# Time-mixing units of a hybrid RWKV-7 / Conformer trunk: key tiles made for both heads at once, chunk-end scaling and row moves on ScalarE, bonus in one matmul

## The chip, the cores and the metric

The kernel runs on one core of one Trainium2 chip. The metric is the device time of one execution in microseconds; lower is better. Before the change it is 2194.57 us, the median of three runs.

## The reference, cut to what matters

The program is a two-layer trunk over 512 tokens of width 1024. Each layer is a SwiGLU feed-forward block, a mixer, and another feed-forward block; the first mixer is RWKV-7 time mixing, the second a causal convolution module. The change touches time mixing alone: for each of 16 heads of 64 channels a 64 x 64 state S is carried through the tokens.

```python
kk = k * k_k, normalised per head
k  = k * (1 + (a - 1) * k_a)
a_vec, b_vec = -kk, kk * a
# per token t and head:
sa = S @ a_t
S  = S * w_t + outer(sa, b_t) + outer(v_t, k_t)
y_t = S @ r_t
# after the scan:
y = group_norm(y) * ln_gain + ln_bias
bonus = sum(r * k * r_k over the head) * v
out = ((y + bonus) * g) @ w_out
```

## The kernel before, in words

Activations stand transposed, channels on the 128 partitions and tokens along the free dimension. Large products run on TensorE in fp32r with operands split in a rounded part and a rest (names ending in h and l), three matmuls for each product. Weights come by DMA in tiles `wr` of eight blocks; ScalarE casts each to `wh`, VectorE makes the rest `wl = wr - wh`, and TensorE uses both. Two buffers of each exist.

Time mixing is cut into eight units. Unit p holds two pairs of heads for one half of the tokens (four chunks of 64 tokens for each pair); units 0 to 3 are the first half of the sequence, 4 to 7 the second. A unit has a front part (tiles for all eight chunks) and a back part (a chain over four chunk steps). Rows 0 to 63 of a tile belong to the first head of a pair, rows 64 to 127 to the second.

Front part: `ka` holds kk and r times the running decay `pt` (a product for each head and each half of the unit, on GpSimd); `bkc` holds b (VectorE) and k (GpSimd) divided by the decay, the two in different column order for the two heads; `bkh` is `bkc` times the decay at the chunk's end `pc` (GpSimd). Matmuls `Gb` and `Gk` of `bkc` and `ka` give the matrices within a chunk; VectorE masks `Gk` into the free rows of `ka`, and inverts the triangular part with many small instructions on `tm` and `lt`, and with matmuls `X` and `D` into `tt`.

Back part: `tk` transposes `bkh` into `bk`; `tv` centres v, and ScalarE puts it into `uv` and `mv`. Each of the four steps is a chain of three groups of matmuls into `z`: from `ka` and `mv`, a copy, from `tt`, two copies into `uv`, from `bk` and `uv`, and an addition into the next columns of `mv`. Then `y` is made from `ka`, `mv`, `Gb` and `uv`. The bonus `bo` is a product with a block-diagonal matrix of ones, from `k2` = r k r_k, which is split in `k2..h` (ScalarE) and `k2..l` (GpSimd), so two fp32r matmuls.

The order of all instructions is fixed before the run by a planner in the kernel (class `Sched`): it lists instructions on the engines from its own table of costs, a due order (the program's order), numbers of buffers, and rules for the port that VectorE and GpSimd share. Where it sees TensorE about to wait it puts in fillers, `warm`: matmuls of 128 x 512 on a constant tile whose result nobody reads. An engine then works strictly in that order; where the chip is slower than the table, the whole queue behind waits. `copier` means that the planner picks ScalarE or VectorE for a copy, `both` VectorE or GpSimd.

Between the steps of units TensorE is given projections (`k`, `r`, `v`), the output projection `wo` and the feed-forward block that follows (`f1g`, `f1u`, `f1d`).

## Time and profile before

| | |
|---|---|
| three runs | 2194.26, 2194.57, 2195.81 us |
| profiled execution: time, span | 2190.93 us, 2189.1 us |
| TensorE busy | 2137.0 us, 98% of the span |
| VectorE busy | 1303.9 us, 60% |
| ScalarE busy | 854.8 us, 39% |
| GpSimd busy | 521.2 us, 24% |
| stretch with the units' steps | 470 to 930 us of the span |

The profiled execution is one run, 0.17% below the median of the three. Busy time of TensorE includes the tail of each pipelined matmul, so a short wait does not show as idle time.

### The profile page before, as it was taken

Reading aid. Unit: us, or ns where it says so; the run is one execution under the profiler, and the core shown is the slowest. Engines: PE = TensorE matmul, PEld = TensorE weight load, DVE = VectorE, ACT = ScalarE, POOL = GpSimd, SP = SyncE. Lnnn points to the kernel's source line nnn. Section 1 sums busy time; section 2 is a strip of 40 time slices with the busy share of each in tenths; the row PEclk is TensorE's granted clock in tenths of the full one; section 3 lists DMA queues with packets and bytes.
Section 4 is the critical chain, followed back from the end, with each engine's and each line's share of the span. In section 5 each row is a group of like instructions: output and inputs, shape, how many; then the busy total and the mean of one; then the engine's idle time right before and its main releaser. Section 6 shows DMA issues by size and latency. Waiting matters only on the chain.

```text
span 2189.1 us, 37961 instructions
## 1 busy us (share of the span) xinstructions
PE 2137.0 (98%) x15539; PEld 1857.8 (85%) x15539; DVE 1303.9 (60%) x2165; ACT 854.8 (39%) x1317; POOL 521.2 (24%) x487
## 2 busy tenths in 40 slices
PE   9999999899989989999999999999999999999998
PEld 7888889678878889899998888888877699988998
DVE  5333447878799898575434443334479878643454
ACT  4222235456644463354223322122321266432343
POOL 2110113463463262031111112021211142211100
PEclk9999999999999999999999999999999999999999
DMA  4333336223224344356333233333245555533465
GB/s 162 96 96 101 93 105 203 67 84 91 70 74 128 102 116 125 116 183 184 109 94 97 88 95 102 96 98 96 90 121 154 145 153 183 182 118 96 135 186 152
DMA packets 120463, 262.20 MB, mean 120 GB/s; under 512 B 47072, under 2 KB 59744, under 8 KB 120288
## 3 DMA queue, kind: packets, MB, share of 16 engines
q1 hardware_dynamic: 86624, 254.52, 38.2%
q10 hardware_dynamic: 33664, 5.25, 1.3%
q8 instruction: 122, 2.00, 0.4%
q14 instruction: 53, 0.43, 0.1%
HBM read 250.19 MB, written 9.54 MB: 119 GB/s over the span
## 4 chain that ended last, share of the span: by engine, by line
PE 86%; DVE 9%; issue 2%; ACT 2%; POOL 1%; DMA 0%; SPq 0%; ACTq 0%; DVEq 0%; POOLq 0%
PE f3d L691 6%; PE f1d L691 6%; PE f0d L691 6%; PE f3g L691 6%; PE f3u L691 6%; PE f2d L691 6%; PE f2g L691 6%; PE f2u L691 6%; PE f0u L691 5%; PE f0g L691 5%; PE f1u L691 5%; PE f1g L691 5%; PE wo L691 2%; PE co L691 2%; PE ca L691 2%
## 5 line engine op out<-in xcount | busy, mean ns | idle before, releaser
L691 ACT CAST wh<-wr 128x1024 fp32r<-128x1024 f32 (+1 forms) x448 | 467.6, 1045 | 1032.2 <-issue 384.0
L691 DVE TENSOR_TENSOR wl<-wr,wh 128x1024 fp32r<-128x1024 f32 (+1 forms) x448 | 556.7, 1244 | 262.4 <-ACT wh L691 254.2
L691 POOL TENSOR_TENSOR f0ss<-f0ss,n0rs 128x512 f32<-128x512 f32 x22 | 39.4, 1789 | 255.5 <-ACT f0ss L691 255.5
L691 POOL TENSOR_TENSOR f2ss<-f2ss,n2rs 128x512 f32<-128x512 f32 x22 | 38.8, 1764 | 249.1 <-ACT f2ss L691 249.1
L691 POOL TENSOR_TENSOR f1ss<-f1ss,n1rs 128x256 f32<-128x256 f32 (+1 forms) x33 | 49.2, 1492 | 205.0 <-ACT f1ss L691 201.8
L691 POOL TENSOR_TENSOR f3ss<-f3ss,n3rs 128x256 f32<-128x256 f32 (+1 forms) x33 | 49.6, 1504 | 193.6 <-ACT f3ss L691 193.6
L691 PE MATMUL f3g<-f_h,wh 128*128 128x256 f32 (+1 forms) x264 | 84.6, 321 | 0.0
L691 PE MATMUL f3u<-f_h,wh 128*128 128x256 f32 (+1 forms) x264 | 84.6, 320 | 0.0
L691 PE MATMUL f3g<-f_l,wh 128*128 128x256 f32 (+1 forms) x264 | 84.4, 320 | 0.0
L691 PE MATMUL f3u<-f_l,wh 128*128 128x256 f32 (+1 forms) x264 | 84.4, 320 | 0.0
L691 PE MATMUL f3g<-f_h,wl 128*128 128x256 f32 (+1 forms) x264 | 84.2, 319 | 0.0
L691 PE MATMUL f3u<-f_h,wl 128*128 128x256 f32 (+1 forms) x264 | 84.2, 319 | 0.0
L691 DVE SCALAR_TENSOR_TENSOR dwa<-ch,dw,dwa 128x256 f32<-128x256 f32 (+10 forms) x160 | 72.5, 492 | 1.0
L691 PE MATMUL f0g<-f_2h,wh 128*128 128x512 f32 x176 | 69.6, 396 | 1.2 <-ACT wh L691 1.2
L691 PE MATMUL f0g<-f_2l,wh 128*128 128x512 f32 x176 | 69.9, 397 | 0.7 <-DVE f_2l L691 0.7
L691 PE MATMUL f2u<-f_2l,wh 128*128 128x512 f32 x176 | 69.6, 396 | 0.0
L691 PE MATMUL f2g<-f_2l,wh 128*128 128x512 f32 x176 | 69.6, 395 | 0.0
L691 PE MATMUL f0u<-f_2h,wl 128*128 128x512 f32 x176 | 69.6, 395 | 0.0
L691 PE MATMUL f0u<-f_2h,wh 128*128 128x512 f32 x176 | 69.4, 395 | 0.0
L691 PE MATMUL f0g<-f_2h,wl 128*128 128x512 f32 x176 | 69.4, 394 | 0.0
L691 PE MATMUL f0u<-f_2l,wh 128*128 128x512 f32 x176 | 69.4, 394 | 0.0
L691 PE MATMUL f2u<-f_2h,wh 128*128 128x512 f32 x176 | 69.3, 394 | 0.0
(1507 smaller groups left out, 6737.3 us busy)
## 6 DMA issues: line engine op xcount, KB each, us to landing
wr<-wst SPq DMA_DIRECT2D x444, 512.0 KB, 3.5
hr<-hd SPq DMA_DIRECT2D x64, 65.0 KB, 2.0
hr<-hd SPq DMA_DIRECT2D x64, 61.2 KB, 2.0
x<-xT SPq DMA_DIRECT2D x8, 256.0 KB, 5.6
xspill<-x SPq DMA_DIRECT2D x8, 256.0 KB, 5.3
dl<-Gb ACTq DMA_DIRECT2D x16, 128.0 KB, 2.2
t<-dt ACTq DMA_DIRECT2D x8, 256.0 KB, 3.1
xr<-xspill SPq DMA_DIRECT2D x8, 256.0 KB, 5.1
```

What stands on the lines that cost most here:

```text
L691: self.tc.keep_in_program_order(getattr(eng, m)(*op.args, **op.kw))
```

## The change

The a, r, b and k tiles are computed for both heads in one instruction over 128 partitions, with the same column order for both. So GpSimd issues 4 products for `ka` in a unit instead of 8, and 2 for `bkc` instead of 4; VectorE issues 2 instead of 4. `ka` of the second head, which the masked `Gk` must share with it, is filled by a ScalarE copy of 64 rows, two in a unit. `bkh` is made by eight ScalarE multiplications of 128 columns instead of two GpSimd products of 512. As b now stands in the same rows of `bk` for both heads, u of the second head has to be in rows 0 to 63 of `uv` for the state and in rows 64 to 127 (a new tile, `u1`) for the output: three copies in a chunk step instead of two. The bonus is one fp32 matmul with the constant itself, without a split.

```diff
-BOR = 1
+BOR = 0
...
         for i in range(2):
             cc = slice(4 * i, 4 * i + 4)
-            for h in range(2):
-                o = own[h]
-                gp.tensor_tensor(ka[h][i][o, :, 0, :], c3(kk)[o, cc], pt[o, cc, :CH], ALU.mult)
-                gp.tensor_tensor(ka[h][i][o, :, 1, :], c3(r)[o, cc], pt[o, cc, 1:], ALU.mult)
+            gp.tensor_tensor(ka[0][i][:, :, 0, :], c3(kk)[:, cc], pt[:, cc, :CH], ALU.mult)
+            gp.tensor_tensor(ka[0][i][:, :, 1, :], c3(r)[:, cc], pt[:, cc, 1:], ALU.mult)
+            act.copy(ka[1][i][own[1]], ka[0][i][own[1]])
...
-        ob = (slice(0, CH), slice(CH, P))
-        ok = (slice(CH, P), slice(0, CH))
+        ob = (slice(0, CH), slice(0, CH))
+        ok = (slice(CH, P), slice(CH, P))
...
-            for h in range(2):
-                o = own[h]
-                vec.scalar_tensor_tensor(bkc[i][o, :, ob[h]], c3(bt)[o, cc], -0.5, c3(ni)[o, cc],
-                                         ALU.mult, ALU.mult)
+            vec.scalar_tensor_tensor(bkc[i][:, :, ob[0]], c3(bt)[:, cc], -0.5, c3(ni)[:, cc],
+                                     ALU.mult, ALU.mult)
...
-            for h in range(2):
-                o = own[h]
-                gp.tensor_tensor(bkc[i][o, :, ok[h]], c3(k2)[o, cc], c3(ni)[o, cc], ALU.mult)
+            gp.tensor_tensor(bkc[i][:, :, ok[0]], c3(k2)[:, cc], c3(ni)[:, cc], ALU.mult)
...
-            gp.tensor_tensor(bkh[i].rearrange("p (c x) -> p c x", x=P), bkc[i],
-                             pc[:, 4 * i:4 * i + 4].unsqueeze(2).broadcast_to([P, NC // 2, P]), ALU.mult)
+            for ci in range(NC // 2):
+                act.mul(bkh[i][:, ci * P:ci * P + P], bkc[i][:, ci], pc[:, 4 * i + ci:4 * i + ci + 1])
...
-                           KA(h, c)[own[h]], start=True, stop=True)
+                           KA(0, c)[own[h]], start=True, stop=True)
...
-            act.copy(UV[h][oth[h]], ps[oth[h]])
+            act.copy(UV[h][oth[0]], ps[oth[h]])
...
-                    self.s.after("gpsimd", bkh[1])
+                    self.s.after("gpsimd", bkc[1])
...
-            for h in range(2):
-                nc.copier.copy(two(UV[h], cc)[own[h]], both(1, own[h]))
+            nc.copier.copy(two(UV[0], cc)[own[0]], both(1, own[0]))
+            act.copy(two(UV[1], cc)[own[0]], both(1, own[1]))
+            nc.copier.copy(two(U1, cc)[own[1]], both(1, own[1]))
...
-                mm(py[o, sl], UV[h][o, sl], G(gb, c, 1)[o], start=False, stop=c == NC - 1,
+                mm(py[o, sl], UO[h][o, sl], G(gb, c, 1)[o], start=False, stop=c == NC - 1,
```

The planner makes a new order from this, on every engine from unit 0 on. In the lists below a line of the kernel stands first (L691 is the helper that emits nearly everything), then the operation, what it writes and reads, and the shape; the digit after a tile's name is the unit, a last number is the planner's count.

GpSimd, front part of unit 4, before:

```order
L691 TENSOR_TENSOR ka00_4_1158<-ru4_706,pt_4_1153 64x4x64
L691 TENSOR_TENSOR ka10_4_1160<-kk_4_1157,pt_4_1153 64x4x64
L691 TENSOR_TENSOR ka10_4_1160<-ru4_706,pt_4_1153 64x4x64
L691 TENSOR_TENSOR ka01_4_1159<-kk_4_1157,pt_4_1153 64x4x64
L691 TENSOR_TENSOR ka11_4_1161<-kk_4_1157,pt_4_1153 64x4x64
L691 TENSOR_TENSOR ka01_4_1159<-ru4_706,pt_4_1153 64x4x64
L691 TENSOR_TENSOR ka11_4_1161<-ru4_706,pt_4_1153 64x4x64
L691 COPY pc4_1162<-pt_4_1153 128x8
L691 TENSOR_TENSOR bkc0_4_1164<-k2_4_1166,ni_4_1154 64x4x64 x2
L691 TENSOR_TENSOR bkc1_4_1165<-k2_4_1166,ni_4_1154 64x4x64 x2
L691 TENSOR_TENSOR bkh0_4_1167<-bkc0_4_1164,pc4_1162 128x512
L691 TENSOR_TENSOR bkh1_4_1168<-bkc1_4_1165,pc4_1162 128x512
```

and the same place of the changed kernel:

```order
L691 TENSOR_TENSOR ka00_4_1155<-kk_4_1154,pt_4_1150 128x4x64
L691 TENSOR_TENSOR ka01_4_1156<-kk_4_1154,pt_4_1150 128x4x64
L691 TENSOR_TENSOR ka00_4_1155<-ru4_706,pt_4_1150 128x4x64
L691 TENSOR_TENSOR ka01_4_1156<-ru4_706,pt_4_1150 128x4x64
L691 COPY pc4_1159<-pt_4_1150 128x8
L691 COPY mv0_4_1349<-carry_588 64x64 x2
L691 COPY mv1_4_1350<-carry_588 64x64 x2
L691 TENSOR_TENSOR bkc0_4_1161<-k2_4_1163,ni_4_1151 128x4x64
L691 TENSOR_TENSOR bkc1_4_1162<-k2_4_1163,ni_4_1151 128x4x64
```

The products are half as many and twice as tall, and `bkh` is gone from this queue.

ScalarE of the changed kernel, where the front part of unit 4 meets the first steps of unit 2's chain (tiles `z2`, `uv0_2`, `uv1_2`, `u1_2`):

```order
L691 CAST wh109_1184<-wr109_1183 128x1024
L691 COPY ka10_4_1157<-ka00_4_1155 64x512
L691 COPY ka11_4_1158<-ka01_4_1156 64x512
L691 COPY z3_0_1261<-z3_0_1260 128x128
L691 COPY uv0_2_1094<-z2_0_1098 64x2x64
L691 COPY uv1_2_1095<-z2_0_1098 64x2x64
L691 COPY u1_2_1097<-z2_0_1098 64x2x64
L691 ACTIVATE bkh0_4_1164<-bkc0_4_1161,pc4_1159 128x128 x4
L691 CAST wh110_1189<-wr110_1188 128x1024
L691 ACTIVATE bkh1_4_1165<-bkc1_4_1162,pc4_1159 128x128 x4
```

The row copies of `ka` and the multiplications of `bkh` stand in the queue between a chain's copies and the casts of weights; before, this place held only casts, copies and the issue of DMAs.

TensorE at the third step of unit 6's chain (`z6_2`), before:

```order
L691 MATMUL z6_2_1630<-mv1_6_1620,ka11_6_1414 64x64
L758 MATMUL warm107_11058<-idr_88 128x512
L758 MATMUL warm108_11060<-idr_88 128x512
L758 MATMUL warm109_11062<-idr_88 128x512
L691 MATMUL f1u10_0_1687<-f1_0h0_0_1340,wh148_1685 128x256
L691 MATMUL f1u10_0_1687<-f1_0l0_0_1341,wh148_1685 128x256
L691 MATMUL z6_2_1630<-z6_2_1631,tt_6_1431 64x64 x4
L758 MATMUL warm110_11074<-idr_88 128x512
L758 MATMUL warm111_11076<-idr_88 128x512
L691 MATMUL f1u10_0_1687<-f1_0h0_0_1340,wl148_1686 128x256
```

and of the changed kernel:

```order
L691 MATMUL z6_2_1623<-mv1_6_1614,ka11_6_1409 64x64
L691 MATMUL z7_1_1656<-mv0_7_1648,ka00_7_1453 64x64
L691 MATMUL z7_1_1656<-mv1_7_1649,ka10_7_1455 64x64
L691 MATMUL z7_1_1656<-mv0_7_1648,ka01_7_1454 64x64
L691 MATMUL z7_1_1656<-mv1_7_1649,ka11_7_1456 64x64
L691 MATMUL f1g10_0_1675<-f1_0h0_4_1340,wh147_1639 128x256
L691 MATMUL f1g10_0_1675<-f1_0l0_4_1341,wh147_1639 128x256
L691 MATMUL z6_2_1623<-z6_2_1624,tt_6_1426 64x64 x4
L691 MATMUL z7_1_1656<-z7_1_1657,tt_7_1473 64x64 x4
L691 MATMUL f1g10_0_1675<-f1_0h0_4_1340,wl147_1640 128x256
```

The fillers are gone there, and unit 7's chain runs beside unit 6's. Over the program the fillers are 95 before and 93 after: from unit 0's chain to the start of the second `wo`, with the three that follow just behind it, 43 before and 23 after; at the layer norms of the convolution module 5 before and 16 after (5 of them in front of the second half's `co` matmuls, where there were none); at the very end none before and 7 after.

## Rows read from the trace of the kernel before

**Rows 1.** The page: busy time by engine, and the chain that ended last.

```profile
PE 2137.0 (98%) x15539; PEld 1857.8 (85%) x15539; DVE 1303.9 (60%) x2165; ACT 854.8 (39%) x1317; POOL 521.2 (24%) x487
...
PE 86%; DVE 9%; issue 2%; ACT 2%; POOL 1%; DMA 0%; SPq 0%; ACTq 0%; DVEq 0%; POOLq 0%
```

**Rows 2.** Windows: length, then busy us (instructions) of PE, PEld, DVE, ACT, POOL.

```profile
470.00:930.00 460.00, 435.19 (x5124) 380.50 (x5122) 377.47 (x857) 230.26 (x431) 179.17 (x215) 1.00 0.36 102
570.00:670.00 100.00, 87.09 (x1123) 72.85 (x1124) 91.55 (x208) 45.54 (x92) 49.67 (x67) 1.00 0.28 73
```

**Rows 3.** The same window, the fillers alone: length, busy us (instructions).

```profile
470.00:930.00 460.00, 14.52 (x43) 1.00 0.36 102
```

**Rows 4.** TensorE's waits, 470 to 930 us: total us, times, longest.

```profile
PE v L691 <- DVE wl L691: 6.8, 7, 2.5
PE f1u L691 <- DVE wl L691: 3.9, 2, 3.7
PE z L691 <- DVE mv L691: 2.8, 5, 1.0
...
PE X L691 <- DVE ti L691: 1.7, 1, 1.7
...
PE z L691 <- DVE uv L691: 0.7, 1, 0.7
```

**Rows 5.** Timeline of GpSimd at 807 us: start, us, instruction.

```profile
807.60 1.42 POOL L691 TENSOR_TENSOR ka<-ru,pt 64x256 f32<-64x256 f32 x2
809.09 0.72 POOL L691 TENSOR_TENSOR f1ss<-f1ss,n1rs 128x256 f32<-128x256 f32 x1
```

**Rows 6.** Timeline of VectorE in the same stretch and behind it.

```profile
809.10 0.77 DVE L691 TENSOR_TENSOR lt<-lt,tm 64x39 f32<-64x39 f32 x1
...
813.17 0.21 DVE L691 TENSOR_TENSOR lt<-lt,tm 64x60 f32<-64x60 f32 x1
```

**Rows 7.** GpSimd's groups, 470 to 930 us: count | busy, mean ns | idle before.

```profile
L691 POOL TENSOR_TENSOR bkc<-k,ni 64x256 f32<-64x256 f32 x32 | 30.4, 951 | 23.6 <-DVE k L691 14.9 <-DVE lt L691 7.0
L691 POOL TENSOR_TENSOR ka<-kk,pt 64x256 f32<-64x256 f32 x30 | 29.2, 973 | 31.2 <-DVE ti L691 13.2 <-ACT pt L691 11.6 <-issue 4.0
L691 POOL TENSOR_TENSOR ka<-ru,pt 64x256 f32<-64x256 f32 x31 | 24.9, 803 | 1.6
L691 POOL TENSOR_TENSOR bkh<-bkc,pc 128x512 f32<-128x512 f32 x16 | 16.9, 1074 | 0.7
...
L691 POOL TENSOR_TENSOR k24l<-k,k24h 128x512 fp32r<-128x512 f32 x1 | 1.3, 1286 | 3.0 <-ACT k24h L691 3.0
```

**Rows 8.** VectorE's groups, 470 to 930 us.

```profile
L691 DVE TENSOR_TENSOR wl<-wr,wh 128x1024 fp32r<-128x1024 f32 x75 | 97.0, 1297 | 23.9 <-ACT wh L691 23.4
...
L691 DVE SCALAR_TENSOR_TENSOR bkc<-bt,ni 64x256 f32<-64x256 f32 x28 | 16.2, 580 | 0.7
```

**Rows 9.** ScalarE's groups, 470 to 930 us.

```profile
L691 ACT COPY uv<-z 64x128 f32<-64x128 f32 x52 | 13.5, 259 | 21.3 <-PE z L691 16.8 <-PE Gb L691 2.4 <-PE Gk L691 1.7
L691 ACT COPY uv<-tv 64x512 f32<-64x512 f32 x16 | 9.3, 581 | 5.6 <-PE tv L691 4.9 <-DVE lt L691 0.5
...
L691 ACT ACTIVATE mt<-xn,om 128x256 f32<-128x256 f32 x15 | 6.9, 504 | 0.0
```

**Rows 10.** Timeline of TensorE at 1241 us: fp32r beside plain fp32 matmuls.

```profile
1241.28 0.40 PE L691 MATMUL f2u<-f_2l,wh 128*128 128x512 f32 x1
1241.51 1.05 PE L691 MATMUL n22bc<-cst,n2ry 128*128 128x128 f32 x8
1242.32 0.48 PE L691 MATMUL f2u<-f_2h,wl 128*128 128x512 f32 x1
```

**Rows 11.** Timeline of TensorE at the first layer norm of the convolution.

```profile
1742.18 4.49 PE L691 MATMUL dwx<-hr,dg 128*32 128x256 f32 x40
1746.61 1.15 PE L691 MATMUL ln0bc<-cst,ly 128*128 128x128 f32 x4
```

**Rows 12.** Timeline of VectorE there: the last result that `ln0bc` needs.

```profile
1744.66 0.16 DVE L691 SCALAR_TENSOR_TENSOR ly<-ra,ly 128x2 f32<-128x2 f32 x1
```

More of the change, by code (lines that the diff above doesn't have):

```diff
@@ L1392, in unit @@
         self.gate[p] = d
+        U1 = S("u1")
+        UO = (UV[0], U1)
         two = lambda t, c: t.rearrange("p (i x) -> p i x", i=2)[:, :, c * CH:c * CH + CH]
```

## The prediction

> **What bounds the kernel now.** The page comes first. TensorE is busy for 2137.0 of 2189.1 us, and 86% of the chain that ended last is TensorE's, 9% VectorE's [rows 1]. So work taken off other engines counts only where TensorE waits for it. The windows say where that is: from 470 to 930 us, the stretch of the units, TensorE is busy for 435.19 of 460 us, 24.8 us idle; 12.9 of these lie between 570 and 670 us, where VectorE is busy for 91.55 of 100 us and ScalarE for 45.54 [rows 2]. In the same stretch stand 43 fillers [rows 3], matmuls that do no work of the program. The table of waits names who is late: VectorE's rest of the weights, `wl`, for 6.8 and 3.9 us, and its additions into `mv`, its `ti` and its copies into `uv` for 2.8, 1.7 and 0.7 us, together 15.9 us [rows 4]. What the reader is to see: there are at most 24.8 us of visible waits and some 10 us of fillers to win, and VectorE holds the larger part.
>
> Why VectorE is late shows in one place. At 809.10 an instruction on `lt` takes 0.77 us, and it ends when GpSimd's instruction that began at 809.09 has ended; a little later, with GpSimd idle, its larger sister takes 0.21 us [rows 5, 6]. The next `wl` stands behind it, and TensorE's wait of 3.7 us is for that `wl` [rows 4].
>
> **The change, part by part.** All sums are against the profiled execution's 2190.93 us, which is 3.6 us (0.17%) under the median of 2194.57 us; I add the change to the median.
>
> *Bonus.* Two fp32r matmuls of 512 columns become one plain fp32 matmul. An fp32r one takes 0.23 us from start to start (1241.28 to 1241.51), so two take 0.46 us; the fp32 product of 4 x 128 columns takes 0.81 us (1241.51 to 1242.32) [rows 10]. That is 0.35 us more, for eight units 2.8 us, on TensorE's own queue: **+2.8**. The Trainium skill, in "FP8 and Floating Point Precision" (TensorE Precision Notes), says that true fp32 takes four passes through the array; by four times the fp32r time the term would be 8 x 0.46 = +3.7 us, an estimate from that page's factor.
>
> *GpSimd.* It loses half of the `ka` products, whose 61 in this window cost 54.1 us, half of the `bkc` products (30.4 us), all of `bkh` (16.9 us) and eight `k2..l` (1.29 us in the row shown, at least 10.3 us) [rows 7]: some 27 + 15 + 17 + 10 = 69 of its 179 us [rows 2]. A product over 128 rows costs no more than one over 64: 128 x 256 took 0.72 us, two of 64 x 256 took 1.42 us [rows 5]. TensorE's long waits are for VectorE, not for GpSimd [rows 4]; so the worth of this lies in what VectorE gets back.
>
> *VectorE.* It loses 14 of 28 `bkc` instructions of 580 ns in the window, 8.1 us [rows 8], and the waits behind the 69 us of GpSimd that are gone. From below these give back nothing, if the port is free by chance; from above 69 us, if VectorE stood behind each of them. The pair of rows above is a wait of half a microsecond behind one instruction of 0.72 us. What TensorE can gain from it is bounded by its 15.9 us of waits for VectorE: between 0 and 15.9. I take half, because half of the `ka` and `bkc` instructions stay: **-8.0**.
>
> Here a rule weighs. "SBUF — State Buffer" (Who interferes with whom) in the Trainium skill says that VectorE and GpSimd share one pair of ports by an exclusive lock that is held for a whole instruction, and not by dividing bandwidth. By the lock the number of GpSimd instructions counts and -8.0 stands; if bandwidth were divided, taller products would press as before, and only `bkh` and `k2..l` would count, 27 of 179 us or 15% of 15.9, which is -2.4 and a sum of -0.6. The rows above, where the late instruction ends with GpSimd's, agree with the lock.
>
> *ScalarE.* It gets 64 multiplications of 128 columns (below 504 ns, that of 256 columns), 16 row copies of 64 x 512 (near 581 ns) and 32 more copies out of `z` (259 ns) [rows 9], and loses eight casts of `k2`. That is up to 32 + 9 + 8, less 5, some 45 us on an engine that is busy for 230 of 460 us [rows 2]. The multiplications and row copies are costed at nothing: they lie between the front part and the back part of a unit, and ScalarE's free 230 us cover them; without that cover they cost up to their 41 us, and the casts `wh` stand behind them. The third copy of each step is in the chain, between two groups of `z`: at worst 32 x 0.26 = 8.3 us, at best nothing, since `u1` is not needed before `y` and comes last of the three. The chains have TensorE work between their steps, but the copies into `uv` were already waited for once, for 0.7 us [rows 4]; I take a third, **+2.5**.
>
> *Fillers.* Those of the units fall from 43 to 23. A filler has the shape of the fp32r matmul at 0.23 us [rows 10], so 20 fewer are worth between 0 (if the place is then idle) and 4.6 us. The order shows what stands there now: a second chain's matmuls, which are work. I take **-4.6**.
>
> *Convolution's layer norms.* The new order shifts things there too. Before, `ln0bc` was ready when `ly` was done (1744.66 + 0.16) and began at 1746.61, behind 40 `dwx` matmuls of 4.49 us [rows 11, 12]. Now nine fillers stand before it, and part of `dwx` behind. At best the norm comes 1.8 us earlier, at worst the 4.49 us are paid later; I take 0. In the second half five fillers stand on TensorE's path before the matmuls of `co`, which had none: 5 x 0.23 = **+1.2**. The seven at the end stand in a wait.
>
> The sum is 2.8 - 8.0 + 2.5 - 4.6 + 1.2 = -6.1 us: 2184.8 for a profiled execution, 2188.5 us for the median.
>
> **The rivals.**
> *No change, because the relief does not arrive.* VectorE's `wl` is itself idle for 23.9 us before it starts, 23.4 of them waiting for ScalarE's `wh` [rows 8], and `wh` now has more in front of it. If the 10.7 us of waits for `wl` stay, only half of the other 5.2 go: 2.8 - 2.6 + 2.5 - 4.6 + 1.2 = -0.7, or 2193.9 us. Against it: at the longest of these waits `wl` stood behind VectorE's own small instructions, held by GpSimd [rows 4 to 6].
> *Slower, because ScalarE's queue stops.* The row copies of `ka` wait for GpSimd, and they stand right in front of the chain copies of another unit, for which TensorE waits in order. Whatever GpSimd is late, the chain is late. A `ka` product takes 0.97 us in the mean [rows 7] against 0.71 alone [rows 5], so four are easily 1 us later than planned, with the products of another unit ahead of them more. At 1.5 us uncovered for each of eight units it costs 12 us: 2200.5 us. It decides against the change from (6.1 + 4.4) / 8 = 1.3 us for each unit. For it speaks the order shown; against it, that ScalarE is half idle and that GpSimd has fewer queues ahead of it than before.
> *More than forecast.* If nearly all 15.9 us go and the chain copies cost nothing, the sum is 2.8 - 15.9 - 4.6 + 1.2 = -16.5, 2178.1 us.
>
> **How the numbers follow.** The forecast, a gain of 4.4 to 15 us: 0.52. More than that: 0.06. No change, within 4.4 us: 0.26. Slower: 0.16. A difference of 0.2%, 4.4 us, is about what a measurement of this kernel tells from none. So faster 0.58, same 0.26, slower 0.16. For the range: below 2177 us only the whole of the waits and more would lead (0.04), and above 2199 most of the slower case (0.14); 2177 to 2199 holds the rest. The faster cases alone lie between 2177 and 2190.
>
> **What would show it.** In the changed profile, TensorE's visible idle time between unit 0's chain and the second `wo` falls from 24.8 to about 17 us, and its waits for `wl` from 10.7 to about 5; the mean of `wl` falls from 1297 ns toward that of its shortest, and GpSimd's busy time in the stretch from 179 to some 110 us. `bo` takes 0.35 us more in each unit. ScalarE is busy for about 270 of 460 us. The forecast is wrong if TensorE's waits turn to `uv`, `z` or `wh` from ScalarE in the place of those for VectorE, if ScalarE's own waits are for `ka` of GpSimd, or if the idle time stays though VectorE's busy time falls.

## The result, and the profile after

The changed kernel takes 2173.51 us in the median of four runs (2171.45 to 2174.79); the kernel before, on the same chip, 2194.41 us (2191.19 to 2195.81). The ratio is 0.9906, with a 95% interval from 0.9889 to 0.9923: faster by 0.94%, 20.9 us between the medians. The forecast was 6.1 us with a range of 2177 to 2199 us, so the sign was right, the size was a third, and the measured time lies below the range. The profiled execution of after took 2174.79 us (span 2173.0 us), the highest of its four runs, and that of before 2190.93 us, below all four of its runs, so the two traces differ by only 16.1 us; the accounts below are of this pair.

Busy time by engine, from the page of the changed kernel (before: [rows 1]):

```profile
PE 2135.3 (98%) x15537; PEld 1858.1 (86%) x15537; DVE 1279.1 (59%) x2161; ACT 885.1 (41%) x1409; POOL 451.0 (21%) x415
```

The stretch of the units as in [rows 2], then its fillers alone as in [rows 3]:

```profile
470.00:930.00 460.00, 446.27 (x5240) 394.67 (x5239) 366.57 (x872) 270.63 (x541) 113.45 (x149) 1.00 0.38 109
...
470.00:930.00 460.00, 8.44 (x23) 3.77 (x23) 1.00 0.38 109
```

TensorE is idle for 13.7 us of the 460 instead of 24.8, and GpSimd is busy for 113 us instead of 179. First starts of TensorE's groups show where the gain arises: `k`, just ahead of the units, starts at 384.5 us before and 384.0 after; `f2g`, behind the units and the feed-forward block, at 1231.1 and 1215.2; `ca`, at the convolution's start, at 1599.8 and 1584.7; `f3d`, near the end, at 2051.2 and 2035.4. So 15.4 us of it arise between `k` and `f2g`, where the units are, and nothing of weight before or after. In this pair TensorE's clock hides 2.8 us more of it; the section on the prediction shows the rows.

TensorE's waits there, 470 to 930 us (before: [rows 4]):

```profile
PE v L691 <- DVE wl L691: 3.1, 3, 1.3
PE z L691 <- DVE mv L691: 2.9, 5, 0.9
PE D L691 <- DVE xs L691: 2.2, 1, 2.2
PE a L691 <- DVE wl L691: 1.1, 1, 1.1
...
PE z L691 <- ACT z L691: 0.6, 2, 0.4
PE f1g L691 <- DVE wl L691: 0.5, 1, 0.5
PE z L691 <- ACT uv L691: 0.5, 2, 0.3
```

The waits for `wl` are 4.7 us instead of 10.7. No wait for ScalarE has taken their place: those for `z` and `uv` together are 1.1 us. GpSimd's groups in the stretch (before: [rows 7]), VectorE's ([rows 8]) and ScalarE's ([rows 9]):

```profile
L691 POOL TENSOR_TENSOR ka<-ru,pt 128x256 f32<-128x256 f32 x16 | 15.8, 1000 | 0.0
L691 POOL TENSOR_TENSOR bkc<-k,ni 128x256 f32<-128x256 f32 x16 | 14.9, 948 | 8.6 <-DVE lt L691 3.2 <-DVE tm L691 2.7 <-DVE k L691 2.7
L691 POOL TENSOR_TENSOR ka<-kk,pt 128x256 f32<-128x256 f32 x15 | 14.7, 995 | 48.3 <-issue 20.1 <-ACT pt L691 19.2 <-PE z L691 9.0
```

```profile
L691 DVE TENSOR_TENSOR wl<-wr,wh 128x1024 fp32r<-128x1024 f32 x80 | 100.6, 1259 | 30.9 <-ACT wh L691 30.4
...
L691 DVE SCALAR_TENSOR_TENSOR bkc<-bt,ni 128x256 f32<-128x256 f32 x14 | 6.0, 453 | 0.1
```

```profile
L691 ACT COPY ka<-ka 64x512 f32<-64x512 f32 x16 | 9.8, 616 | 2.6 <-POOL ka L691 2.3
```

A GpSimd product of 128 rows takes 0.95 to 1.00 us in the mean, little more than one of 64 rows took (0.80 to 0.97), so half as many take little more than half the time. ScalarE's row copies wait 2.3 us in all for GpSimd's `ka`, so its queue does not stop there.

The bonus on TensorE's timeline at 566 us:

```profile
566.20 1.02 PE L691 MATMUL bo<-k,cst 128*128 128x512 f32 x2
566.66 0.68 PE L691 MATMUL v<-mx_0h,wh 128*128 128x256 f32 x1
567.18 0.28 PE L691 MATMUL v<-mx_0l,wh 128*128 128x256 f32 x1
```

One fp32 matmul of 512 columns leaves two records. The next matmul's record starts 0.46 us after the first of them, but that is not the price: this `v` lasts 0.68 us where its neighbour lasts 0.28, so it stood behind the bonus. The one after it starts 0.98 us after the bonus began; less the 0.12 us from one `v` to the next, the bonus takes 0.86 us, near the 0.81 of the forecast.

### The profile page after: what moved, and what is told of

It reads as the page before. It is cut to its first block, busy times and chain, and to the rows that moved or that the text cites. A ratio compares the mean times of both kernels' runs of the same rounds, so it can differ in the third digit from the quotient of the medians.

```text
span 2173.0 us, 37947 instructions
## 1 busy us (share of the span) xinstructions
PE 2135.3 (98%) x15537; PEld 1858.1 (86%) x15537; DVE 1279.1 (59%) x2161; ACT 885.1 (41%) x1409; POOL 451.0 (21%) x415
## 4 chain that ended last, share of the span: by engine, by line
PE 88%; DVE 8%; ACT 2%; issue 1%; DMA 1%; SPq 0%; POOL 0%; ACTq 0%; DVEq 0%; POOLq 0%
PE f3d L691 6%; PE f0d L691 6%; PE f3u L691 6%; PE f1d L691 6%; PE f2d L691 6%; PE f2u L691 6%; PE f2g L691 6%; PE f1g L691 6%; PE f3g L691 6%; PE f0u L691 5%; PE f0g L691 5%; PE f1u L691 5%; PE co L691 2%; PE wo L691 2%; PE ca L691 2%; PE k L691 2%
## 5 line engine op out<-in xcount | busy, mean ns | idle before, releaser
L691 ACT CAST wh<-wr 128x1024 fp32r<-128x1024 f32 (+1 forms) x448 | 467.6, 1045 | 1028.7 <-issue 384.6
L691 DVE TENSOR_TENSOR wl<-wr,wh 128x1024 fp32r<-128x1024 f32 (+1 forms) x448 | 553.4, 1236 | 268.9 <-ACT wh L691 259.8
L691 POOL TENSOR_TENSOR f1ss<-f1ss,n1rs 128x256 f32<-128x256 f32 (+1 forms) x33 | 47.3, 1436 | 244.5 <-ACT f1ss L691 222.7
L691 POOL TENSOR_TENSOR f0ss<-f0ss,n0rs 128x512 f32<-128x512 f32 x22 | 39.4, 1792 | 255.5 <-ACT f0ss L691 255.5
L691 POOL TENSOR_TENSOR f2ss<-f2ss,n2rs 128x512 f32<-128x512 f32 x22 | 39.0, 1772 | 250.1 <-ACT f2ss L691 250.1
L691 POOL TENSOR_TENSOR f3ss<-f3ss,n3rs 128x256 f32<-128x256 f32 (+1 forms) x33 | 48.8, 1478 | 187.0 <-ACT f3ss L691 180.5
L691 PE MATMUL f3u<-f_h,wl 128*128 128x256 f32 (+1 forms) x264 | 84.4, 320 | 0.4 <-DVE wl L691 0.4
L691 PE MATMUL f3g<-f_l,wh 128*128 128x256 f32 (+1 forms) x264 | 84.2, 319 | 0.0
L691 PE MATMUL f3u<-f_l,wh 128*128 128x256 f32 (+1 forms) x264 | 84.2, 319 | 0.0
L691 PE MATMUL f3g<-f_h,wl 128*128 128x256 f32 (+1 forms) x264 | 84.2, 319 | 0.0
L691 PE MATMUL f3g<-f_h,wh 128*128 128x256 f32 (+1 forms) x264 | 83.9, 318 | 0.0
L691 PE MATMUL f3u<-f_h,wh 128*128 128x256 f32 (+1 forms) x264 | 83.9, 318 | 0.0
L691 DVE SCALAR_TENSOR_TENSOR dwa<-ch,dw,dwa 128x256 f32<-128x256 f32 (+10 forms) x160 | 72.5, 494 | 1.1
L691 PE MATMUL f0g<-f_2h,wh 128*128 128x512 f32 x176 | 69.6, 396 | 1.5 <-ACT wh L691 1.3
L691 PE MATMUL f0g<-f_2l,wh 128*128 128x512 f32 x176 | 70.0, 397 | 0.7 <-DVE f_2l L691 0.7
L691 PE MATMUL f2u<-f_2h,wl 128*128 128x512 f32 x176 | 69.6, 395 | 0.0
L691 PE MATMUL f0u<-f_2h,wl 128*128 128x512 f32 x176 | 69.5, 395 | 0.0
L691 PE MATMUL f0g<-f_2h,wl 128*128 128x512 f32 x176 | 69.5, 395 | 0.0
L691 PE MATMUL f0u<-f_2h,wh 128*128 128x512 f32 x176 | 69.4, 395 | 0.0
L691 PE MATMUL f2g<-f_2h,wl 128*128 128x512 f32 x176 | 69.4, 394 | 0.0
L691 PE MATMUL f2u<-f_2h,wh 128*128 128x512 f32 x176 | 69.4, 394 | 0.0
L691 PE MATMUL f2g<-f_2h,wh 128*128 128x512 f32 x176 | 69.4, 394 | 0.0
```

The lines of the kernel that those rows point to most:

```text
L691: self.tc.keep_in_program_order(getattr(eng, m)(*op.args, **op.kw))
```

## The experiments

Eighteen kernels were run, each beside the kernel before on the same chip; each ratio is to that. Where a run is set against the changed kernel, the difference is (its ratio - 0.9906) x 2194 us; the interval of one ratio is some 3 us to either side, that of a difference of two ratios some 4 to 5 us. There are two kinds. In a *same-order* run the planner's list is untouched, and only the code that emits it (`emit`) issues something else at a place of it; nothing else moves. A *replanned* run is a changed program, for which the planner makes a new order.

### What a new order is worth by itself

```diff
-    PH = 0.0
+    PH = 0.4
```

On the changed kernel:

> The changed kernel with one number of the planner moved (the phase of its model of TensorE's clock, PH, 0.4 us instead of 0): the same work in an order planned anew, to see what a new order is worth by itself. Theory A (the gain is in what the change takes off GpSimd and VectorE): within 4 us of the changed kernel, 2170 to 2178 us. Theory B (the gain is a lucky order): 5 us or more slower.

2176.19 us, ratio 0.9916 (0.9904 to 0.9929): 2.2 us slower, within the interval. On the kernel before:

> The kernel before with the planner's PH at 0.4 us instead of 0: the same work in an order planned anew. If the order of before was an unlucky one (theory B): 5 us or more faster than before. If not: within 4 us, as with the changed kernel, 2190 to 2198 us.

2189.61 us, ratio 0.9983 (0.9974 to 0.9991): 3.7 us faster, beyond it. So two new orders of the same work moved the time by 2.2 and 3.7 us, and theory B, luck alone, may account for a part of the 20.9 us but not for most of it. Replanned runs below are read with this margin, though two samples do not bound it.

### The parts of the change

The bonus alone, in the kernel before (`BOR = 0`), and split again in the changed kernel (`BOR = 1`):

> The kernel before with the bonus in one fp32 matmul alone, planned anew. By the prediction's price 2.8 us on TensorE, against eight GpSimd instructions of 1.3 to 2.4 us that go: at the 0.4 us that each us of GpSimd cost with bkh there, 5 us back: 2 us faster than before, 2190 to 2193 us. By the prediction's sum (2.8 less 10 of 69 us of 8.0): 1.6 us slower, 2195 us. If an order planned anew is worth more than such prices: anywhere within 8 us.

2192.11 us, ratio 0.9999 (0.9989 to 1.0009): no difference. If TensorE pays 8 x 0.40 us for it, as the timeline at 566 us has it, the release of GpSimd or the new order gives that back; the run does not tell which.

> The changed kernel with the bonus in two fp32r matmuls and the split of k2 again, planned anew. By the prediction's prices: 2.8 us less on TensorE, and eight more GpSimd instructions of 1.3 to 2.3 us, which by theory A cost 1.5 to 3 us through VectorE: 0 to 1 us faster, 2172.5 to 2173.5 us. If plain fp32 is dearer than the 0.35 us taken: over 3 us faster, under 2171 us. If the new order's worth is what decides (theory B): anywhere within 8 us to either side.

2180.21 us, ratio 0.9941 (0.9928 to 0.9954): 7.7 us slower, a miss of every price. TensorE has less to do in it, so what costs is the eight GpSimd instructions and ScalarE casts, or a new order; the run does not tell these apart.

`bkh` alone, on ScalarE in the kernel before, and everything but that in the changed kernel:

```diff
-            gp.tensor_tensor(bkh[i].rearrange("p (c x) -> p c x", x=P), bkc[i],
-                             pc[:, 4 * i:4 * i + 4].unsqueeze(2).broadcast_to([P, NC // 2, P]), ALU.mult)
+            for ci in range(NC // 2):
+                act.mul(bkh[i][:, ci * P:ci * P + P], bkc[i][:, ci], pc[:, 4 * i + ci:4 * i + ci + 1])
```

> The kernel before with one part of the change alone: bkh made by eight ScalarE multiplications of 128 columns a unit in the place of two GpSimd products, planned anew. By the price that the idle products gave (5.0 us for 18.9 us of GpSimd), 16.9 us less on GpSimd: 4 to 5 us faster than before, 2188 to 2190 us. If the moved work then holds ScalarE up: within 2 us of before.

2190.31 us, ratio 0.9988 (0.9979 to 0.9997): 2.6 us faster than before, less than the 4 to 5 expected and within the margin of a new order.

> The changed kernel without that part: bkh stays two GpSimd products a unit; the tiles for both heads at once, the row copies, the third copy and the whole bonus stay; planned anew. By the price of the idle products 5 us slower than the changed kernel, 2177 to 2180 us, so that the rest of the change is worth 14 to 16 us. If the whole gain came with bkh: near 2193 us.

2175.81 us, ratio 0.9919 (0.9906 to 0.9932): 17.8 us faster than before, 2.9 us slower than the changed kernel, which is within the interval. So most of the gain comes without `bkh`. As the whole bonus alone is worth nothing in the kernel before, this points to the tiles made for both heads at once; it does not show it by itself, for the parts do not simply add, as the 7.7 us of the split bonus show.

### Does a GpSimd product hold VectorE up?

Behind ScalarE's last `bkh` multiplication of each half, GpSimd gets work whose result nobody reads, once as the product of before, once as two memsets of the same length:

```diff
+                    d = self.dum.rearrange("p (c x) -> p c x", x=P)
+                    self.tc.keep_in_program_order(self.nc.gpsimd.tensor_tensor(d, s, c, ALU.mult))
```

```diff
+                    for _ in range(2):
+                        self.tc.keep_in_program_order(self.nc.gpsimd.memset(self.dum, 0.0))
```

> The changed kernel in its own order, bkh on ScalarE as in the change, and behind it two more GpSimd products of 128 x 512 a unit (bkc times pc, as before the change) into a tile that nobody reads: 16 of some 1.1 us, 18 us. Theory A (such a product holds VectorE up): 5 to 8 us slower than the changed kernel, 2179 to 2182 us, as with bkh itself on GpSimd, and TensorE's waits for VectorE grow. Theory D (with bkh on GpSimd it was bkh that came late, or its place in the chain): within 2 us of the changed kernel, 2172 to 2176 us.

2178.52 us, ratio 0.9926 (0.9913 to 0.9939): 4.4 us slower, at the edge of the interval.

> As the run with idle products, but in the place of each product two memsets of 128 x 512 into the tile that nobody reads, 0.52 us each by the profile, so the same 17 us of GpSimd's queue without two operands to read. Theory A (what counts is that a product with two operands shares its way to SBUF with VectorE): within 2 us of the changed kernel. Theory E (GpSimd's queue itself: its later products come late, ka and k above all): as slow as the idle products.

2172.07 us, ratio 0.9900 (0.9888 to 0.9913): 1.3 us faster, no difference. The two ran side by side, and all five runs with products (2176.49 us and more) are slower than all four with memsets (2175.85 us and less), by 5.7 us from ratio to ratio. Both orders are the same, so one place can be looked at in both. With products, GpSimd and then VectorE:

```profile
626.09 2.22 POOL L698 TENSOR_TENSOR dum<-bkc,pc 128x512 f32<-128x512 f32 x2
```

```profile
626.12 1.29 DVE L692 SCALAR_TENSOR_TENSOR k<-ru,vec,k 128x256 f32<-128x256 f32 x1
627.33 1.00 DVE L692 SCALAR_TENSOR_TENSOR gr<-ra,gr 128x8 f32<-128x8 f32 x1
```

With memsets:

```profile
626.18 2.29 POOL L698 MEMSET dum<- 128x512 f32 x4
```

```profile
626.20 0.48 DVE L692 SCALAR_TENSOR_TENSOR k<-ru,vec,k 128x256 f32<-128x256 f32 x1
626.60 0.16 DVE L692 SCALAR_TENSOR_TENSOR gr<-ra,gr 128x8 f32<-128x8 f32 x1
```

The two products last from 626.09 to 628.31. `k` takes 1.29 us and ends at 627.41, just behind the first product; `gr`, eight columns wide, takes 1.00 us and ends at 628.33, just behind the second. Beside memsets the same two take 0.48 and 0.16 us. This is theory A, shown: 18.9 us of products whose result nobody reads cost 4.4 us, 16.8 us of memsets in their place nothing.

The same idle work, each product issued as two of 64 rows:

```diff
-                    self.tc.keep_in_program_order(self.nc.gpsimd.tensor_tensor(d, s, c, ALU.mult))
+                    for o in (slice(0, CH), slice(CH, P)):
+                        self.tc.keep_in_program_order(self.nc.gpsimd.tensor_tensor(d[o], s[o], c[o], ALU.mult))
```

> As the run with idle products, each of them issued as two of 64 rows: 32 of some 1.1 us, the same data, 36 us of GpSimd. If VectorE is held up for as long as each of GpSimd's instructions lasts (the number counts): twice the 5.0 us, 9 to 11 us slower than the changed kernel, 2182 to 2185 us. If the two share a bandwidth (the data count): as the idle products, 2177 to 2180 us.

2184.65 us, ratio 0.9966 (0.9953 to 0.9978): 13.2 us slower where the same data in half as many instructions cost 4.4; the forecast for a price by number was twice, and the data alone would have left it at 4.4. GpSimd and VectorE of this run:

```profile
622.52 4.44 POOL L699 TENSOR_TENSOR dum<-bkc,pc 64x512 f32<-64x512 f32 x4
```

```profile
622.54 1.30 DVE L692 SCALAR_TENSOR_TENSOR k<-ru,vec,k 128x256 f32<-128x256 f32 x1
623.76 1.00 DVE L692 SCALAR_TENSOR_TENSOR gr<-ra,gr 128x8 f32<-128x8 f32 x1
624.69 0.68 DVE L692 TENSOR_TENSOR Gb<-Gb,cst 128x512 f32<-128x512 f32 x1
```

VectorE's instructions on 128 rows wait as long for a product on 64 rows as for one on 128 (`k` 1.30 and 1.29 us, `gr` 1.00 us in both). The pages of the three runs say the same of the whole program; memsets, products and half products:

```profile
PE 2137.2 (98%) x15537; PEld 1860.9 (86%) x15537; DVE 1280.7 (59%) x2161; ACT 884.7 (41%) x1409; POOL 467.7 (22%) x447
PE 2137.2 (98%) x15537; PEld 1860.1 (85%) x15537; DVE 1287.6 (59%) x2161; ACT 885.2 (41%) x1409; POOL 470.3 (22%) x431
PE 2137.2 (98%) x15537; PEld 1858.8 (85%) x15537; DVE 1296.0 (59%) x2161; ACT 885.6 (41%) x1409; POOL 487.9 (22%) x447
```

VectorE's same 2161 instructions are busy for 6.9 us more with 16 products than with memsets, and for 15.3 us more with 32 half products. So the count of GpSimd's products is what VectorE pays for, not their data. That is the exclusive lock of the Trainium skill, "SBUF — State Buffer" (Who interferes with whom), and these runs agree with it. `Gb`, which reads PSUM, takes 0.68 us beside a product, no more than elsewhere. The 13.2 us of time may hold something besides: the half products make GpSimd's queue 18.6 us longer than the whole ones do (37.5 for 18.9), and no run put that much more of memsets at this place.

### Undoing the merge, with the order kept

GpSimd's 48 products for `ka` and `bkc` in halves:

```diff
+            if op.eng == "gpsimd" and m == "tensor_tensor" and tuple(op.args[0].shape) == (P, 4, CH):
+                for o in (slice(0, CH), slice(CH, P)):
+                    a = [x[o] if isinstance(x, bass.AP) else x for x in op.args]
+                    self.tc.keep_in_program_order(getattr(eng, m)(*a, **op.kw))
+                continue
```

> The changed kernel in its own order on every engine; only GpSimd's products for ka and for k in bkc are issued as two of 64 rows, as before the change: 96 for 48, some 35 to 45 us more on GpSimd at 0.7 to 0.95 us each. Theory A (TensorE waited for VectorE, and VectorE for GpSimd, by the number of GpSimd's instructions): about half of the gain is lost, 5 to 9 us slower than the changed kernel, 2178 to 2183 us, and TensorE's waits for VectorE in the stretch of the units come back. Theory B (the gain is in the new order that the planner found, with two units' chains side by side, and not in what GpSimd holds up on the chip): within 2 us of the changed kernel, 2172 to 2176 us.

2203.54 us, ratio 1.0048 (1.0035 to 1.006): 31.2 us slower than the changed kernel and slower than before, far over what either theory gave. ScalarE's waits in the stretch:

```profile
ACT ka L696 <- POOL ka L694: 34.0, 15, 4.0
```

and TensorE's:

```profile
PE Gk L696 <- POOL bkc L694: 4.7, 6, 1.2
PE z L696 <- ACT mv L696: 3.0, 2, 2.2
...
PE z L696 <- ACT uv L696: 2.6, 2, 2.3
PE z L696 <- ACT u L696: 2.6, 1, 2.6
PE f1g L696 <- ACT wh L696: 2.4, 2, 2.1
```

This is the mechanism of the prediction's slower rival: the row copy of `ka` stops ScalarE's queue until GpSimd has the products, and behind it stand `uv`, `u`, `mv` and `wh`, for which TensorE waits; `Gk` waits for GpSimd's `bkc` itself. It is real; products half as many keep it away. The run that has the same length of queue without products:

```diff
+            if op.eng == "gpsimd" and m == "tensor_tensor" and tuple(op.args[0].shape) == (P, 4, CH):
+                self.tc.keep_in_program_order(self.nc.gpsimd.memset(self.dum, 0.0))
```

> The changed kernel in its own order; ahead of each of GpSimd's 48 products for ka and k in bkc stands a memset of 128 x 768 into a tile that nobody reads, some 0.76 us each, so that GpSimd's queue is as long as with products in halves (30 us slower), but nobody reads through it. Theory F (what counts is how late ka and k come out of GpSimd's queue, for ScalarE's row copies and TensorE's Gk wait for them): 20 to 30 us slower than the changed kernel, 2193 to 2203 us, with ScalarE's waits for ka of 25 us or more. Theory A (what counts is VectorE held up by products): under 6 us slower, 2174 to 2179 us.

2180.9 us, ratio 0.9951 (0.9937 to 0.9965): 9.9 us slower, between the two theories. ScalarE's waits:

```profile
ACT ka L693 <- POOL ka L693: 17.4, 13, 3.2
```

So of the 31.2 us, 9.9 come with late `ka` and `bkc` alone (the memsets are 0.74 us each, a little shorter than a half product, so this is a lower bound). The other 21 come only when the added time is products, and three things go with them. ScalarE's wait for `ka` doubles, from 17.4 to 34.0 us. VectorE is held up: it is busy for 1290.3 us over the program with halves, for 1279.3 with memsets and 1279.1 in the changed kernel. And TensorE's clock is lower; from the first `r` to the end of `wo`, TensorE alone, halves and then memsets:

```profile
439.70:963.90 524.20, 496.03 (x5403) 0.97 0.35 102
439.20:940.40 501.20, 480.56 (x5403) 1.00 0.37 106
```

The same 5403 matmuls are busy for 15.5 us longer at a granted clock of 0.97, which is 1.2 instead of 2.4 GHz for some 31 of the 524 us; so the clock can hold up to about 15 of the 21 us, an estimate from these rows. The shares were not separated.

VectorE's 16 products for b in halves, in the same way:

```diff
+            if op.eng == "vector" and op.args[0].tensor.name.startswith("bkc"):
```

> The changed kernel in its own order; only VectorE's 16 products for b in bkc are issued as two of 64 rows, as before the change: 16 more of 0.45 us, 7 to 9 us of VectorE. If VectorE's time is what TensorE waits for: 3 to 6 us slower than the changed kernel, 2176 to 2180 us. If there is room for it: within 2 us.

2180.17 us, ratio 0.9943 (0.9931 to 0.9956): 8.1 us slower. The group and TensorE's waits:

```profile
L694 DVE SCALAR_TENSOR_TENSOR bkc<-bt,ni 64x256 f32<-64x256 f32 x28 | 15.6, 557 | 0.5
```

```profile
PE v L696 <- DVE wl L696: 5.1, 4, 2.9
...
PE f1u L696 <- DVE wl L696: 2.4, 1, 2.4
PE a L696 <- DVE wl L696: 1.1, 1, 1.1
PE f1g L696 <- DVE wl L696: 0.7, 1, 0.7
```

9.6 us more on VectorE in the stretch (15.6 for 6.0) cost 8.1: in this fixed order VectorE's time is worth nearly its whole on TensorE, and the waits for `wl` are 9.3 us instead of 4.7.

`bkh` back on GpSimd, with the order kept (at the place of the last of its four multiplications):

> The changed kernel in its own order; only bkh is made by two GpSimd products of 128 x 512 a unit, as before the change, at the place of the last of four ScalarE multiplications, which are gone. 16 more on GpSimd of 1.07 us, 17 us; 64 fewer on ScalarE of 389 ns, 20 to 25 us. Theory A (GpSimd holds VectorE up): 2 to 4 us slower, 2176 to 2178 us. Theory B (the order): within 2 us, 2172 to 2176 us. Theory C (the changed kernel is now held by ScalarE): 1 to 3 us faster, 2171 to 2173 us.

2181.29 us, ratio 0.9942 (0.9929 to 0.9956): 7.9 us slower, more than theory A's 2 to 4, though ScalarE is busy for 248.07 us of the stretch instead of 270.63. The gain of theory C is not there: whatever ScalarE gets back is less than what the products on GpSimd cost.

### Fillers and the third copy

The 20 fillers between unit 0's chain and the second `wo` left out, order kept:

```diff
             if op is None:
+                if self.units:
+                    continue
```

> The changed kernel in its own order, without the 20 fillers between unit 0's chain and the second wo (no result depends on them). If a filler costs its 0.23 us, as the prediction's term of -4.6 us for 20 fewer has it: 4.6 us faster, 2169 us. If fillers stand where TensorE would wait anyway: within 1 us, 2173 to 2175 us, with 4 to 5 us more idle time of TensorE in the stretch. If they keep the clock up: slower, with a granted clock under 1.00 in the stretch.

2173.74 us, ratio 0.9905 (0.9892 to 0.9919): no difference. The window of the units:

```profile
470.00:930.00 460.00, 443.25 (x5229) 393.04 (x5227) 367.36 (x873) 271.63 (x543) 113.65 (x150) 1.00 0.39 110
```

TensorE is idle for 16.75 us instead of 13.7 at the same granted clock, and the time is the same: these fillers cost little or nothing, they stand in waits.

The chain's copy of the second head issued twice, order kept:

```diff
+            if m == "copy" and op.eng == "scalar" and op.args[0].tensor.name.startswith("uv1") and op.args[1].tensor.name.startswith("z"):
+                self.tc.keep_in_program_order(eng.copy(*op.args))
```

> The changed kernel in its own order; in each of the 32 chain steps the ScalarE copy of u's second head into uv is issued twice, 0.26 us more before the third copy. If a third copy in the chain costs what the prediction took (+2.5 us, a third of 8.3): 2 to 3 us slower, 2175 to 2177 us; if every one is on the path: 8.3 us slower, 2182 us; if chains have TensorE work beside them that covers it: within 1 us of the changed kernel.

2174.72 us, ratio 0.9912 (0.9898 to 0.9925): 1.3 us slower, within the interval. TensorE's waits for the copies:

```profile
PE z L691 <- ACT u L691: 2.6, 9, 0.4
...
PE z L691 <- ACT uv L693: 1.1, 2, 0.6
```

These waits are 3.7 us, where the changed kernel has 0.5 for `uv`. The median shows hardly any of it, but the traces do: from the first `r` to the end of `wo` this run takes 496.7 us and the changed kernel 492.9, at a granted clock of 0.99 and 1.00 (rows in the section on the prediction). So the run does not rule out a price of 2 to 3 us.

### Can it be beaten?

Copies moved from GpSimd to ScalarE (`mv` from the carried state, `lt` from the constant), replanned:

```diff
-                    gp.tensor_copy(o, self.carry[own[h], pr * CH:pr * CH + CH])
+                    act.copy(o, self.carry[own[h], pr * CH:pr * CH + CH])
...
-        gp.tensor_copy(tb.rearrange("p a b -> p (a b)"), self.c("id16")[:P // 2])
+        act.copy(tb.rearrange("p a b -> p (a b)"), self.c("id16")[:P // 2])
```

> The changed kernel with two more things moved from GpSimd to ScalarE, planned anew: the copies of the carried state into mv (16 of 0.39 us in the stretch) and of the constant into lt (8 of 0.42 us), 9 us of GpSimd. If copies hold VectorE up as products do: 2 to 3 us faster than the changed kernel, 2170 to 2172 us. If like memsets they don't, or ScalarE's queue pays: no faster, 2172 to 2178 us.

2185.7 us, ratio 0.9965 (0.9952 to 0.9979): 12.9 us slower, a miss by far more than either new order gave. Its longest wait of TensorE in the stretch is one for a DMA, which the changed kernel's table does not have:

```profile
PE X L691 <- DMA t<-dt: 3.6, 1, 3.6
```

No wait is long enough to explain the whole, and the cause stays open.

The decay of the state, `mv` times `pc`, moved from VectorE to ScalarE, for both heads and for one:

```diff
-                    vec.tensor_tensor(
-                        d, two(MV[h], cc)[o], pc[o, cc::NC // 2].unsqueeze(2).broadcast_to([CH, 2, CH]), ALU.mult)
+                    for i in range(2):
+                        act.mul(d[:, i], two(MV[h], cc)[o][:, i], pc[o, cc + 4 * i:cc + 4 * i + 1])
```

> The changed kernel with the decay of the carried state (mv times pc, 60 instructions of 64 x 128 on VectorE, 48 of them in the stretch at 342 ns, 16.4 us) on ScalarE, as two multiplications of 64 x 64 each, some 0.25 to 0.3 us; planned anew. If VectorE's time is worth what the halves of bkc showed, up to 16 us; with an order planned anew a third of that, 4 to 6 us faster than the changed kernel, 2167 to 2170 us. If ScalarE, with 25 to 35 us more on 270 of 460, now holds up wh and the chain: 2 us or more slower, 2176 us or more.

2171.92 us, ratio 0.9908 (0.9895 to 0.9922).

> As the run before, for the second head of each pair alone: 8 us off VectorE, 12 to 17 us on ScalarE. By the same reasoning 2 to 3 us faster than the changed kernel, 2170 to 2172 us, or, if ScalarE holds, 1 us or more slower.

2174.18 us, ratio 0.9914 (0.99 to 0.9927). Neither differs from the changed kernel. For both heads, the window:

```profile
470.00:930.00 460.00, 444.58 (x5219) 393.19 (x5219) 354.57 (x816) 299.29 (x647) 111.10 (x146) 0.99 0.37 108
```

VectorE is busy for 12 us less, and TensorE's idle time does not fall, 15.4 us. Its waits for `wl` are down to 1.0 us, but the casts `wh` that come from ScalarE, 0.4 us in the changed kernel's `v`, are waited for instead:

```profile
PE v L691 <- ACT wh L691: 3.6, 6, 1.2
```

So ScalarE took some of what VectorE gave back, and the two runs do not say what VectorE's time alone is worth in a new order. No version was faster than the changed kernel by more than the interval.

## Why the prediction was wrong in size

Its stretch was right: in the pair of traces the gain arises where the units are. Its direction and its first reason, GpSimd's instructions holding VectorE up by their number, are shown by the idle products, memsets and half products. The signs that it named mostly came: waits for `wl` near 5 us (4.7), GpSimd's busy time near 110 us (113), ScalarE at 270 us (270.6), hardly a wait for ScalarE or for `ka`. The mean of `wl` fell only from 1297 to 1259 ns, 3 us for all of them; the small instructions ahead of it gave back more, those on `lt` (120 in the stretch, 284 ns before and 223 after) 7.5 us.

The steps that failed are terms of the sum:

- *VectorE's waits, -8.0, and fillers, -4.6.* The two are one term. Leaving the fillers out gave nothing, so a filler is a wait that the page counts as busy. The windows over the same work, from the first `k` to the first `r` and from there to the end of `wo`, TensorE alone, before:

```profile
384.50:439.70 55.20, 46.34 (x241) 0.97 0.20 61
439.70:950.30 510.60, 485.15 (x5423) 1.00 0.36 104
```

  and after:

```profile
384.00:442.00 58.00, 50.21 (x241) 0.88 0.18 56
442.00:934.90 492.90, 478.95 (x5403) 1.00 0.38 108
```

  Together 565.8 us have become 550.9, 14.9 less. But the first window, with the same 241 matmuls, is 2.8 us longer after, and that is not the change. The granted clock in it is 0.88 instead of 0.97: TensorE ran at the lower of its two levels, 1.2 instead of 2.4 GHz, for some 10 us more, behind the same waits (2.7 us for `mx_0h`, 0.9 for `mx_7l`, 1.0 for `wh`) in both traces. Other runs have it the other way round; `chain_copy_twice`, in the changed kernel's order, and `before_bonus_whole`:

```profile
384.40:439.60 55.20, 45.55 (x241) 1.00 0.19 59
439.60:936.30 496.70, 480.61 (x5403) 0.99 0.38 107
...
384.50:442.50 58.00, 50.24 (x241) 0.88 0.18 57
```

  So 17.7 us are gained from `r` on, and the clock of this one run hides 2.8 of them. In that second window visible idle time falls from 25.5 to 14.0 us, by 11.5; 20 fillers of 0.23 us are another 4.6; and busy time falls by 6.2 us although the bonus adds 3.2, which leaves, by subtraction, 4.8 us of shorter waits that the page counted as busy. That is 20.9 us of waits (by chance the figure of the medians), where the forecast, its third copy counted in, had 8.0 + 4.6 - 2.5 = 10.1. The step that failed is the bound: "what TensorE can gain from it is bounded by its 15.9 us of waits for VectorE", of which half was taken. In the table VectorE's waits did fall by about that half, from 15.9 to 9.8 us. What the bound left out are the waits for ScalarE's `gr` and `wh`, which fell from 2.2 and 3.0 us to none and 1.2, and the waits that no table names, under fillers and in busy time.
- *Third copy, +2.5.* Doubling a chain copy cost 1.3 us by the medians, with an interval that holds both nothing and the 2.5, and up to 3.8 us by the windows above. So the term is not refuted, and it is not what failed.
- *Bonus, +2.8.* The price holds: by the timeline 0.86 - 0.46 = 0.40 us, eight times 3.2, between the forecast and the +3.7 that it worked out from the Trainium skill's four passes ("FP8 and Floating Point Precision", TensorE Precision Notes); 0.86 is 3.7 times the 0.23 us of an fp32r matmul, so the trace agrees with that page. What the forecast did not credit to it by itself is GpSimd's eight instructions, which may pay it back.
- *Layer norms, +1.2.* From the start of `ca` to that of `f3d` the gain grew from 15.1 to 15.8 us. The granted clock behind `ca` was 0.98 before and 0.99 after, so the term is too small to be read from this pair.

The step from the pair's 16.1 us to the 20.9 of the medians is for 2.8 us this clock; the rest lies in the runs' own spread, before's profiled run being faster than its others and after's slower. The forecast added its sum to a median, as if both profiled runs stood alike.

Two small slips stand in its working and move nothing: with bandwidth divided its sum is -0.5, not -0.6, and the 0.97 us of a `ka` product is that of the `kk` products alone, those of r took 0.80 [rows 7].

Of the rivals, *no change* fell: `wl` still waits 30.4 us for `wh`, yet TensorE's waits for it halved. *Slower* fell, but its mechanism is live, as the halves showed. *More than forecast*, put at 0.06 and -16.5 by its numbers, is what happened in size, but not by its way: the waits named for VectorE did not nearly all go, and that the copies are free is not shown.

What stays open is how much of the 17.8 us that come without `bkh` is the release of VectorE, how much VectorE's own 14 instructions less in the stretch, and how much that units' front parts come out of GpSimd sooner. Prices taken in a fixed order (31 us for GpSimd's halves, of which at least 9.9 are lateness and up to 15 the clock, and 8 for VectorE's) add to more than the gain; that a planned order hides part of what it knows beforehand would explain this, but no run shows it. Some 2 to 4 us may be the luck of an order.

## What to carry to other kernels

Count GpSimd's products of two SBUF operands, not their rows or bytes: each can hold up VectorE's next instruction until it ends (`gr`, 1.00 us for 0.16), so products over half the partitions should be joined into one over all, even where that costs copies on a half-idle ScalarE. Fillers are waits in disguise: add them to an engine's idle time before bounding what can be won. Compare the granted clock of the same stretch before reading a difference of two traces. And a price measured in a fixed order can be larger than what the same work costs once the order is made anew: `bkh` on GpSimd cost 7.9 us and 2.9 us.

## What was not expected of the hardware

A memset on GpSimd did not hold VectorE up (0.48 us for `k` beside memsets, 1.29 beside products), nor did a product hold up a VectorE instruction that reads PSUM (`Gb`, 0.68 us). A VectorE instruction of eight columns can take 1.00 us instead of 0.16 for nothing but a GpSimd product beside it. The record that follows an fp32 matmul starts before that matmul is done and is longer by the rest (0.68 us for 0.28), so a price read from one start to the next is too low, here by 0.4 us. The same 241 matmuls took 55.2 us in some runs and 58.0 in others, at a granted clock of 0.97 to 1.00 and of 0.88, with either kernel.
